# Two small reorderings in a two-block hybrid model: where 44 convolution taps stand, and how the first input arrives

## The chip, the cores and the metric

The kernel runs on one core of a Trainium2 chip. Five engines run side by side, each with its own list of instructions: TensorE (PE, with its weight loads shown as PEld), VectorE (DVE), ScalarE (ACT), GpSimd (POOL) and SyncE (SP), which here issues the transfers from the large memory. The metric is the time of one execution on the device in microseconds; lower is better. Three executions were timed, and the median counts.

## The reference, cut to what matters

Sequence length is 256, model width 1024, all in float32. Block 1 has two layers; each multiplies x by `w_in` (1024 x 4300 columns), runs three kinds of attention on the result, gates, and multiplies by `w_out`. Block 2 has two layers over 256 latent and 256 context tokens, and each layer adds three branches with their own gates: a convolution module, gated linear attention (GLA), and grouped attention.

```python
def hybrid_layer(x, w_in, ...):                      # block 1, two layers
    h = jnp.einsum('bsd,de->bse', x, w_in)           # the first product of the program
...
def conv_module(val, glu, gate, dw_w, dw_b, ln_g, ln_b, w_o):   # block 2
    u = val * jax.nn.sigmoid(glu)
    u = lax.conv_general_dilated(u, dw_w[:, None, :], ...,      # 31 taps, each channel for itself
                                 feature_group_count=D_CONV) + dw_b
    u = jax.nn.silu(layer_norm_2(u, ln_g, ln_b)) * jax.nn.silu(gate)
    return u @ w_o
```

The convolution has 512 channels and 31 taps. On the chip a tap is one elementwise instruction.

## The kernel before, in words

**Products.** Every float32 matrix is kept as a rounded high part and the rest (`h` and `l`), and a product is three TensorE instructions, h by h, h by l and l by h (`mm3`, lines 163 to 165). `WStream` brings the weights: `_dma` (L120, on SP) loads the next block in a fixed order, `_split` makes the high part on ACT (L133) and the rest on DVE (L134). The blocks are named after their columns: `0A` are the first 460 columns of block 1, layer 0, cut along the contraction at k-tiles `KA = (0, 1, 2, 4, 6, 8)` into five pieces of 1, 1, 2, 2, 2 k-tiles; `0B` is the next group.

**The start.** `load_x` (L1654) issues, for each of the five pieces, the part of x and then the part of `0A` that goes with it, ten transfers in all, of 128 to 512 KB. Behind each pair ACT casts x (`xTh`), then `0A` (`wh_0A`), and DVE makes `xTl` and `wl_0A`. The group A has 48 products of 460 columns: 8 k-tiles, two halves of the tokens, three products each. They start when the first piece has been cast. `setup1` then loads constants (`cst`), and the stream goes on with `0B`.

**The taps.** In block 2, `conv_taps` (L985) is a generator of 124 DVE instructions for a layer: 4 tiles of 128 channels, 31 taps each (L989 the first, L991 the rest), 128 x 512 in layer 0 and 128 x 256 in layer 1. `ucv` is their result. `some_taps(n, anchor)` takes the next n of them and lets them stand on DVE behind `anchor`. Who takes how many is set by two tables:

- `TAPS[l]`: behind each of the score steps of the attention in `scores` (L1033). Layer 0 has eight, so at 20 a step the 124 are used up there.
- `TAPG[l]`: four numbers, per gate of the attention branch (`ag`), per merge of that branch (`m3`/`oa`), per gate of the GLA branch (`gg`, in `gated`, L1256), and per merge of that branch (`m2`/`og`, behind L1291 or L1294).

What is left runs in `conv_finish`, whose transposes (`cvt`) need all of `ucv`.

**The order of layer 0 of block 2.** Attention (scores and weighing, one step per block of 128 tokens and key head), with gate products as filler on TensorE; the `ag` gates with outputs `yag`, and merges `m3`/`oa` (product `yoa`); GLA in two parts, for the context tokens (`gl00..`, `gn00..`) and the latent ones (`gl01..`, `gn01..`), moved up by a priority into the attention's tail; the `gg` gates with `ygg`; merges `m2`/`og` (product `yog`); convolution end; `cg` gates; merges `m1`/`oc`. A scheduler fixes each engine's list from the program's order and the priorities; the lists are then run in order.

Of the kernel before, what the change touches and what calls it, by code (L numbers as in the profile page):

```python
# [66 lines left out]
def units1o():  # L67
    return [(f'O{c}{j}', 2 * j, 2, [(512 * c, 512)]) for c in range(2) for j in range(4)]


def ncols(cols):
    return sum(n for _, n in cols)


def pack(w, units):
    parts = []
    for _, k0, kk, cols in units:
        blk = w.reshape(-1, 128, w.shape[1])[k0:k0 + kk]
# [22 lines left out]
class WStream:  # L101
# [12 lines left out]
    def _dma(self):  # L114
        i = self.nd
        self.nd += 1
        g = self.g
        key, src, off, kk, n = self.table[i]
        t = g.sp.tile([128, kk * n], F32, name=f'wr_{key}', tag='wraw', bufs=g.RAW)
        self.last = self.loads[key] = g.nc.sync.dma_start(t, src[off:off + 128 * kk * n].rearrange("(p n) -> p n", p=128))  # L120
        self.raw[i] = t
        if key in self.hooks:
            self.hooks.pop(key)()

    def _split(self):
        i = self.ns
# [607 lines left out]

TAPS = (20, 19)
TAPG = ((0, 15, 5, 4), (3, 3, 14, 10))


def mod_stream(g, l, W):
# [753 lines left out]
def xT_layout(x):  # L1495
    return np.ascontiguousarray(x.T.reshape(8, 128, 256).transpose(1, 0, 2)).reshape(128, 2048)


def host_arrays(inp):
    h = dict(xt=xT_layout(inp['x'][0]), xtok=inp['x'][0], ctxt=xT_layout(inp['ctx_2'][0]), cst=consts(CST),  # L1500
             par1=par1(inp), par2=par2(inp), rowp=rowpar(inp), wup=wup(inp))
    for i, lst in enumerate(CST1):
        h[f'cst1{i}'] = consts(lst)
    for l in range(2):
        h[f'w1_{l}'] = pack(inp['w_in'][l], units1())
# [18 lines left out]
def width(lst):  # L1524
    return sum(w for _, w in lst)


def setup(ctx, tc, ins):
    g = type('G', (), {})()
    nc = g.nc = tc.nc  # L1530
    g.tc = tc
    cp = g.cp = ctx.enter_context(tc.tile_pool(name="cst", bufs=1))
    g.pp = ctx.enter_context(tc.tile_pool(name="psum", bufs=4, space=PSUM))
    sp = g.sp = ctx.enter_context(tc.tile_pool(name="act", bufs=1))
    g.GM, g.AT, g.RAW, g.WB, g.ROW, g.K8, g.T2, g.UP, g.TE, g.TQ = KN
    g.k8 = lambda shape, name, dt=F32: sp.tile(shape, dt, name=name, tag='k8', bufs=g.K8)
    g.te = lambda shape, name, dt=F32: sp.tile(shape, dt, name=name, tag='te', bufs=g.TE)
    g.tq = lambda shape, name, dt=F32: sp.tile(shape, dt, name=name, tag='tq', bufs=g.TQ)
    g.t2 = lambda shape, name, dt=F32: sp.tile(shape, dt, name=name, tag='t2', bufs=g.T2)
    g.dram = ctx.enter_context(tc.tile_pool(name="dram", bufs=1, space=bass.MemoryType.DRAM))  # L1540
    nosync = mybir.DependencyInfo(mybir.DependencyClass.NoSync, mybir.DependencyReason.DATA)
    sync = mybir.DependencyInfo(mybir.DependencyClass.Sync, mybir.DependencyReason.DATA)
    g.wait = lambda a, b: tc.add_manual_dep(a.ins, b.ins.name, sync, reason="both in one go")
    g.after = lambda a, b: tc.add_manual_dep(a.ins, b.ins.name, nosync, reason="one engine, this order")
    c = cp.tile([128, width(CST)], F32, name="cst")
    g.load_cst = lambda: nc.sync.dma_start(c, ins['cst'])
    v = views(c, CST)
    g.idf, g.ones, g.sel8, g.hm, g.zc = v['ident'], v['ones'], v['sel8'], v['hm'], v['zc']
    g.gmask = v['gmask'].rearrange("p (a t) -> p a t", a=2)
    g.rope2c = v['rope2'].rearrange("p (a t d) -> p a t d", a=2, t=2)  # L1550
    g.idb = cp.tile([128, 128], BF, name="idb")
    return g


def setup1(g, ins, W):
# [3 lines left out]

    def load(nm, lst, more=0):  # L1560
        c = g.sp.tile([128, width(lst) + more], F32, name=nm, tag='up', bufs=g.UP)
        nc.sync.dma_start(c[:, 0:width(lst)], ins[nm])
        v.update(views(c, lst))
        return c

    c = load('cst10', CST1[0], 64)
    g.rope1 = v['rope1'].rearrange("p (t a d) -> p t a d", t=2, a=2)
    g.load_cst()
    nc.vector.tensor_copy(g.idb, g.idf)
    g.causal = c[:, width(CST1[0]):].bitcast(BF)  # L1570

# [80 lines left out]


def load_x(g, ins, W):  # L1654
    nc = g.nc
    x32 = g.k8([128, 8, 256], 'x0T')
    xTh = g.k8([128, 8, 256], 'xTh0', F32R)
    xTl = g.k8([128, 8, 256], 'xTl0', F32R)
    for a, b in zip(KA, KA[1:]):
        ks = slice(a, b)  # L1660
        nc.sync.dma_start(x32[:, ks], ins['xt'].rearrange("p (k t) -> p k t", k=8)[:, ks])
        W._dma()
        nc.scalar.copy(xTh[:, ks], x32[:, ks])
        W._split()
        nc.vector.tensor_sub(xTl[:, ks], x32[:, ks], xTh[:, ks].bitcast(F32))
    return xTh, xTl


# [21 lines left out]
def program(ctx, tc, ins, out, parts=(1, 2)):  # L1690
# [110 lines left out]
```

## Time and profile before

| what | value |
|---|---|
| median of 3 runs | 1201.55 us (1201.11, 1201.55 and 2284.37) |
| the profiled execution | 1202.12 us, its span 1200.3 us |
| PE busy | 1170.1 us, 97% of the span |
| PEld busy | 978.8 us, 82% |
| DVE busy | 919.0 us, 77% |
| ACT busy | 571.1 us, 48% |
| mean granted TensorE clock | 0.995 of full |
| chain that ended last | PE 75%, DVE 13%, DMA 5%, ACT 4%, issue 2% |

The span is cut into stretches, and in each the busy time of every engine is set against the stretch's length. Where TensorE is not busy, the timeline gives in square brackets how long it was idle ahead of an instruction and who ended the wait. The granted clock of a stretch stands as a share of full speed: 0.50 is 1.2 GHz and 1.00 is 2.4 GHz. Matmuls overlap, so the start of one to the start of the next tells their pace, not the duration shown.

### The profile page before, as it was taken

To read this page: it belongs to the slowest core of one execution; us is meant where nothing else is said; L and a number is where in the kernel's file an instruction comes from. 1 tells how busy PE (TensorE), PEld (TensorE's weight loads), DVE (VectorE), ACT (ScalarE), POOL (GpSimd) and SP (SyncE) were. 2 spreads that over 40 slices of the span, in tenths; PEclk is the share of its full clock that TensorE was granted. 3 is DMA by queue.
4 is the path that set the end of the run, shared out by engine and by line. 5 is a ranking of instruction groups with operands and counts; after the bars stand their busy time and mean duration, and the time that the engine had idled before them with its cause. 6 is when DMAs were issued, how large, how long until landed. Compare 5 with 4: busy or idle time off the path is not lost.

```text
span 1200.3 us, 20616 instructions
## 1 busy us (share of the span) xinstructions
PE 1170.1 (97%) x8012; PEld 978.8 (82%) x8012; DVE 919.0 (77%) x2050; ACT 571.1 (48%) x1024; POOL 11.2 (1%) x42
## 2 busy tenths in 40 slices
PE   8999999999999999999799999999999999999998
PEld 6888766677887777778578888888999778999998
DVE  6986766966799759999946544845799897896984
ACT  5556534456565433246254522433455533855552
POOL 0000000000000000000000000000000000000000
PEclk9999999999999999999899999999999999999999
DMA  7643566466555642131131332334655333544552
GB/s 258 230 126 121 191 202 227 166 211 201 188 189 205 197 140 71 44 115 37 57 119 54 93 101 88 88 105 158 177 159 170 110 106 112 187 160 124 176 176 71
DMA packets 48258, 171.33 MB, mean 143 GB/s; under 512 B 5340, under 2 KB 6492, under 8 KB 47392
## 3 DMA queue, kind: packets, MB, share of 16 engines
q1 hardware_dynamic: 48160, 170.01, 43.5%
q8 instruction: 63, 1.03, 0.3%
q14 instruction: 35, 0.29, 0.1%
HBM read 167.89 MB, written 2.10 MB: 142 GB/s over the span
## 4 chain that ended last, share of the span: by engine, by line
PE 75%; DVE 13%; DMA 5%; ACT 4%; issue 2%; SPq 0%; ACTq 0%; DVEq 0%
PE f0m L163 3%; PE f0m L165 3%; PE f0m L164 3%; PE f1m L165 2%; PE f1m L163 2%; PE f1m L164 2%; PE mod L749 1%; PE po L164 1%; PE po L165 1%; PE po L163 1%; PE go L165 1%; PE go L164 1%; PE go L163 1%; DVE ucv L991 1%; PE yog L165 1%
## 5 line engine op out<-in xcount | busy, mean ns | idle before, releaser
L991 DVE SCALAR_TENSOR_TENSOR ucv<-up,par,ucv 128x512 f32<-128x512 f32 (+1 forms) x240 | 146.9, 612 | 2.1
L165 PE MATMUL f0m<-hTh,wl_0m 128*128 128x512 f32 x192 | 75.4, 393 | 0.0
L163 PE MATMUL f0m<-hTh,wh_0m 128*128 128x512 f32 x192 | 75.3, 392 | 0.0
L164 PE MATMUL f0m<-hTl,wh_0m 128*128 128x512 f32 x192 | 75.2, 392 | 0.0
L163 PE MATMUL f1m<-hTh,wh_1m 128*128 128x256 f32 x192 | 54.9, 286 | 0.1
L165 PE MATMUL f1m<-hTh,wl_1m 128*128 128x256 f32 x192 | 54.8, 286 | 0.0
L164 PE MATMUL f1m<-hTl,wh_1m 128*128 128x256 f32 x192 | 54.5, 284 | 0.0
L133 ACT CAST wh_0m<-wr_0m 128x1024 fp32r<-128x1024 f32 x24 | 25.3, 1054 | 58.1 <-PE f0m L164 15.7
L134 DVE TENSOR_TENSOR wl_0m<-wr_0m,wh_0m 128x1024 fp32r<-128x1024 f32 x24 | 29.2, 1220 | 21.6 <-ACT wh_0m L133 21.5
L165 PEld LDWEIGHTS f0m<-hTh,wl_0m 128*128 128x128 f32 x192 | 36.2, 189 | 7.7 <-issue 0.2
L164 PEld LDWEIGHTS f0m<-hTl,wh_0m 128*128 128x128 f32 x192 | 36.2, 189 | 7.4
L163 PEld LDWEIGHTS f0m<-hTh,wh_0m 128*128 128x128 f32 x192 | 36.2, 189 | 7.4
L163 PEld LDWEIGHTS f1m<-hTh,wh_1m 128*128 128x128 f32 x192 | 36.8, 192 | 0.5 <-ACT wh_1m L133 0.3
L165 PEld LDWEIGHTS f1m<-hTh,wl_1m 128*128 128x128 f32 x192 | 36.7, 191 | 0.2 <-DVE wl_1m L134 0.2
L164 PEld LDWEIGHTS f1m<-hTl,wh_1m 128*128 128x128 f32 x192 | 36.8, 191 | 0.1
L133 ACT CAST wh_1m<-wr_1m 128x1024 fp32r<-128x1024 f32 x24 | 25.0, 1050 | 24.4 <-PE f1m L164 9.8
L134 DVE TENSOR_TENSOR wl_1m<-wr_1m,wh_1m 128x1024 fp32r<-128x1024 f32 x24 | 29.3, 1219 | 8.6 <-ACT wh_1m L133 8.4
L1278 ACT ACTIVATE mtm<-f0m,hbin 128x512 f32<-128x512 f32 x24 | 16.4, 682 | 9.3 <-DVE acc L1291 8.9
L134 DVE TENSOR_TENSOR wl_0o<-wr_0o,wh_0o 128x1024 fp32r<-128x1024 f32 x8 | 9.8, 1224 | 13.2 <-ACT wh_0o L133 13.2
L1392 DVE SCALAR_TENSOR_TENSOR xT<-po,mod,xT 128x256 f32<-128x256 f32 x16 | 7.7, 483 | 14.6 <-PE po L165 14.6
L164 PE MATMUL yoa<-yag,wh_0oa 128*128 128x512 f32 x32 | 13.2, 414 | 5.3 <-DVE yag L199 5.3
L164 PE MATMUL po<-mgl,wh_0o 128*128 128x256 f32 x64 | 18.2, 285 | 0.0
(1854 smaller groups left out, 3971.6 us busy)
## 6 DMA issues: line engine op xcount, KB each, us to landing
wr_0mod<-in_wm_dram SPq DMA_DIRECT2D x24, 512.0 KB, 4.4
wr_1mod<-in_wm_dram SPq DMA_DIRECT2D x24, 512.0 KB, 3.6
wr_0m<-in_w_dram SPq DMA_DIRECT2D x24, 512.0 KB, 3.5
wr_1m<-in_w_dram SPq DMA_DIRECT2D x24, 512.0 KB, 3.5
wr_0O<-in_w1o_dram SPq DMA_DIRECT2D x8, 512.0 KB, 3.6
wr_1O<-in_w1o_dram SPq DMA_DIRECT2D x8, 512.0 KB, 4.1
wr_0o<-in_wo_dram SPq DMA_DIRECT2D x8, 512.0 KB, 3.5
wr_0p<-in_wo_dram SPq DMA_DIRECT2D x8, 512.0 KB, 3.7
```

What stands on the lines that cost most here:

```text
L133: g.nc.scalar.copy(wh, r)
L134: g.nc.vector.tensor_sub(wl, r, wh.bitcast(F32))
L163: nc.tensor.matmul(out, lh, rh, start=start, stop=False)
L164: nc.tensor.matmul(out, lh, rl, start=False, stop=False)
L165: nc.tensor.matmul(out, ll, rh, start=False, stop=stop)
L749: nc.tensor.matmul(ps[32 * q:32 * q + 32], g.cz[:, k // 2, 2 * (k % 2):2 * (k % 2) + 32], w[:, 0, 256 * q:256 * q + 256], start=k == 0, st ...
L991: yield nc.vector.scalar_tensor_tensor(o, src, dw[:, i, j:j + 1], o, op0=OP.mult, op1=OP.add)
L1278: nc.scalar.activation(sg, pm, AF.Tanh, scale=0.5, bias=hb[:, blk(n, f)])
L1392: nc.vector.scalar_tensor_tensor(r[:, f, :], ps[:, :256], g.mod[l][:, 16 + f, w:w + 1], r[:, f, :], op0=OP.mult, op1=OP.add)
```

## The change: two tables of numbers, and another way in for the first input

First, `TAPS` for layer 0 of block 2 goes from 20 to 10 and its `TAPG` from (0, 15, 5, 4) to (0, 0, 6, 4). Layer 1 keeps its numbers. There are still 124 taps. Second, x and `0A` are packed on the host piece by piece into one array `xa`; `load_x` brings it in five transfers of 358, 358, 716, 716 and 716 KB, one behind the other in SP's list, into tiles of the pool `k8`, and `take()` hands the weights in them to the stream. The constants' loads are ordered behind them. Third, twelve bf16 products of 128 x 512 on a tile of zeros stand ahead of everything on TensorE; their result is read by nobody. A branch that the program never took is removed.

```diff
-TAPS = (20, 19)
-TAPG = ((0, 15, 5, 4), (3, 3, 14, 10))
+TAPS = (10, 19)
+TAPG = ((0, 0, 6, 4), (3, 3, 14, 10))
...
+def pack_xa(x, w):
+    parts = []
+    for _, k0, kk, cols in units1()[:len(KA) - 1]:
+        blk = pack(w, [('A', k0, kk, cols)]).reshape(128, -1)
+        parts.append(np.concatenate([blk, x[:, 256 * k0:256 * (k0 + kk)]], axis=1).reshape(-1))
+    return np.concatenate(parts)
...
+    def take(self, dma, r):
+        key = self.table[self.nd][0]
+        self.last = self.loads[key] = dma
+        self.raw[self.nd] = r
+        self.nd += 1
...
 def load_x(g, ins, W):
-    x32 = g.k8([128, 8, 256], 'x0T')
+    z = g.te([128, 512], 'z0', BF)
+    nc.vector.memset(z, 0.0)
+    pz = g.pp.tile([128, 512], F32, name='pz0', tag='at', bufs=g.AT)
+    for _ in range(12):
+        nc.tensor.matmul(pz, z[:, 0:128], z, start=True, stop=True)
...
-    for a, b in zip(KA, KA[1:]):
-        ks = slice(a, b)
-        nc.sync.dma_start(x32[:, ks], ins['xt'].rearrange("p (k t) -> p k t", k=8)[:, ks])
-        W._dma()
-        nc.scalar.copy(xTh[:, ks], x32[:, ks])
+    o = 0
+    for j, (a, b) in enumerate(zip(KA, KA[1:])):
+        ks, nw = slice(a, b), (b - a) * NA
+        n = nw + (b - a) * 256
+        r = g.k8([128, n], f'xa{j}')
+        d = nc.sync.dma_start(r, ins['xa'][o:o + 128 * n].rearrange("(p n) -> p n", p=128))
+        if j:
+            g.after(d, W.last)
+        W.take(d, r[:, 0:nw])
+        o += 128 * n
+        x32 = r[:, nw:n].rearrange("p (k t) -> p k t", t=256)
+        nc.scalar.copy(xTh[:, ks], x32)
         W._split()
-        nc.vector.tensor_sub(xTl[:, ks], x32[:, ks], xTh[:, ks].bitcast(F32))
+        nc.vector.tensor_sub(xTl[:, ks], x32, xTh[:, ks].bitcast(F32))
```

The lines move: L134 becomes L155, L199 L220, L991 L1012, L1142 L1163, L1180 L1201 and so on.

DVE, at the end of the attention of layer 0, before: the last `yag`, which `yoa` needs, stands between taps (L991) and the second half of the context GLA (`gl001..`).

```order
L1180 SCALAR_TENSOR_TENSOR sts_5657<-gw_0_5661,gl000dec,gl000c_6308 128x128
L991 SCALAR_TENSOR_TENSOR ucv_4999<-up_4597,par_1328,ucv_4999 128x512
L1137 COPY gl001last<-gl001cum 128x8
L991 SCALAR_TENSOR_TENSOR ucv_4999<-up_4597,par_1328,ucv_4999 128x512
L1142 TENSOR_TENSOR gl001ks_6341<-gl001last,gl001cum 128x512
L991 SCALAR_TENSOR_TENSOR ucv_4999<-up_4597,par_1328,ucv_4999 128x512
L199 SCALAR_TENSOR_TENSOR yag_0_5665<-qag_5663,yag_0_5664 128x512
L991 SCALAR_TENSOR_TENSOR ucv_4999<-up_4597,par_1328,ucv_4999 128x512
L1145 TENSOR_TENSOR gl001ks_6341<-gl001ks_6341,qkT_5380 128x512
```

After, on DVE around the last `yag` (now L220):

```order
L1172 TENSOR_TENSOR gl000ki_6259<-gl000ki_6259,qkT_5344 128x512
L220 SCALAR_TENSOR_TENSOR yag_0_5629<-qag_5627,yag_0_5628 128x512
L155 TENSOR_TENSOR wl_0oa_5897<-wr_0oa_5790,wh_0oa_5896 128x1024
L1198 COPY gw_0_5625<-gl000c_6271 128x256
L1201 SCALAR_TENSOR_TENSOR gw_0_5625<-gw_0_5625,gl000dec,gl000c_6272 128x128 x2
L1201 SCALAR_TENSOR_TENSOR gw_0_5625<-gw_0_5625,gl000dec,gl000c_6271 128x128 x2
L1201 SCALAR_TENSOR_TENSOR sts_5621<-gw_0_5625,gl000dec,gl000c_6272 128x128 x2
L1158 COPY gl001last<-gl001cum 128x8
L1163 TENSOR_TENSOR gl001ks_6305<-gl001last,gl001cum 128x512
L1166 TENSOR_TENSOR gl001ks_6305<-gl001ks_6305,qkT_5344 128x512
L1171 TENSOR_TENSOR gl001qi_6309<-gl001qi_6309,qkT_5344 128x512
```

The taps are gone from this place, and `yag` stands ahead of `gl001last`.

DVE in the `gg` gates, before: each gate is L1253, L1256 and L199, with a weight split (L134) between two gates and no tap.

```order
L1253 SCALAR_TENSOR_TENSOR qgg_6738<-gtgg_0_6772,qgg_6738 128x512
L1256 TENSOR_TENSOR qgg_6738<-qgg_6738,goT_6264 128x512
L199 SCALAR_TENSOR_TENSOR ygg_0_6740<-qgg_6738,ygg_0_6739 128x512
L134 TENSOR_TENSOR wl_0og_6858<-wr_0og_6741,wh_0og_6857 128x1024
L1253 SCALAR_TENSOR_TENSOR qgg_6738<-gtgg_0_6810,qgg_6738 128x512
L1256 TENSOR_TENSOR qgg_6738<-qgg_6738,goT_6264 128x512
L199 SCALAR_TENSOR_TENSOR ygg_0_6740<-qgg_6738,ygg_0_6739 128x512
L134 TENSOR_TENSOR wl_0m_2_6896<-wr_0m_2_6779,wh_0m_2_6895 128x1024
L1253 SCALAR_TENSOR_TENSOR qgg_6738<-gtgg_0_6848,qgg_6738 128x512
```

After, at the same gates:

```order
L1274 SCALAR_TENSOR_TENSOR qgg_6702<-gtgg_0_6736,qgg_6702 128x512
L1277 TENSOR_TENSOR qgg_6702<-qgg_6702,goT_6228 128x512
L220 SCALAR_TENSOR_TENSOR ygg_0_6704<-qgg_6702,ygg_0_6703 128x512
L1012 SCALAR_TENSOR_TENSOR ucv_5168<-up_4541,par_1337,ucv_5168 128x512 x3
L155 TENSOR_TENSOR wl_0og_6841<-wr_0og_6705,wh_0og_6840 128x1024
L1012 SCALAR_TENSOR_TENSOR ucv_5168<-up_4541,par_1337,ucv_5168 128x512
L1274 SCALAR_TENSOR_TENSOR qgg_6702<-gtgg_0_6780,qgg_6702 128x512
L1012 SCALAR_TENSOR_TENSOR ucv_5168<-up_4541,par_1337,ucv_5168 128x512
L1277 TENSOR_TENSOR qgg_6702<-qgg_6702,goT_6228 128x512
L1012 SCALAR_TENSOR_TENSOR ucv_5168<-up_4541,par_1337,ucv_5168 128x512
L220 SCALAR_TENSOR_TENSOR ygg_0_6704<-qgg_6702,ygg_0_6703 128x512
L1012 SCALAR_TENSOR_TENSOR ucv_5168<-up_4541,par_1337,ucv_5168 128x512
```

Six taps follow each gate's output, so they stand ahead of the next gate's.

SP at the start, before, from the ninth transfer on (`x0T` is the last part of x, `wr_0A_109` the last piece of `0A`; the eight ahead are the same pairs):

```order
L1661 DMA x0T<-in_xt_dram 128x512
L120 DMA wr_0A_109<-in_w_0_dram 128x920
L1562 DMA cst_117<-in_cst_dram 128x256
L1546 DMA cst<-in_cst_dram 128x782
L120 DMA wr_0B_145<-in_w_0_dram 128x1024
```

After, from the fourth on:

```order
L1691 DMA xa_110<-in_xa_dram 128x1432
L1691 DMA xa_118<-in_xa_dram 128x1432
L1583 DMA cst_126<-in_cst_dram 128x256
L1567 DMA cst<-in_cst_dram 128x782
L130 DMA wr_0B_154<-in_w_0_dram 128x1024
```

Five transfers (`xa`) stand where ten did, ahead of the same constants and the same `0B`.

## Rows read from the trace of the kernel before

**Rows 1.** the page, parts 1 and 4: busy time by engine; the chain of waits by engine

```profile
PE 1170.1 (97%) x8012; PEld 978.8 (82%) x8012; DVE 919.0 (77%) x2050; ACT 571.1 (48%) x1024; POOL 11.2 (1%) x42
...
PE 75%; DVE 13%; DMA 5%; ACT 4%; issue 2%; SPq 0%; ACTq 0%; DVEq 0%
```

**Rows 2.** stretches of the program: length, busy time (instructions) of each engine, PE clock, DMA share, GB/s

```profile
440.00:571.46 131.46, 131.45 (x985) 102.14 (x985) 125.30 (x212) 57.03 (x92) 3.25 (x7) 1.00 0.21 65
571.46:576.72 5.26, 0.00 (x1) 0.01 (x1) 5.26 (x12) 1.43 (x4) 0.00 (x0) 0.79 0.00 0
576.72:584.65 7.93, 7.68 (x74) 6.43 (x75) 7.93 (x13) 0.96 (x2) 0.00 (x0) 0.50 0.16 39
584.65:610.00 25.35, 21.61 (x166) 17.45 (x165) 20.66 (x40) 9.78 (x25) 0.17 (x2) 1.00 0.38 125
...
656.30:690.40 34.10, 33.77 (x153) 27.64 (x152) 18.89 (x32) 19.34 (x39) 0.00 (x0) 1.00 0.29 84
690.40:747.00 56.60, 56.60 (x258) 47.03 (x256) 22.65 (x26) 15.67 (x18) 0.00 (x0) 1.00 0.31 99
```

**Rows 3.** the timeline, TensorE's first products: start, us, engine line op out<-in [idle before <-releaser]

```profile
4.57 0.75 PE L163 MATMUL g0A<-wh_0A,xTh 128*128 128x460 f32 x1 [4.57 <-ACT wh_0A L133]
...
12.64 0.59 PE L165 MATMUL g0A<-wh_0A,xTl 128*128 128x460 f32 x1
...
13.79 0.59 PE L165 MATMUL g0A<-wh_0A,xTl 128*128 128x460 f32 x1
...
15.05 0.37 PE L165 MATMUL g0A<-wh_0A,xTl 128*128 128x460 f32 x1
...
20.43 0.37 PE L165 MATMUL g0A<-wh_0A,xTl 128*128 128x460 f32 x1
...
21.04 0.19 PEld L164 LDWEIGHTS g0B<-wl_0B,xTh 128*128 128x128 f32 x1 [0.21 <-DVE wl_0B L134]
```

**Rows 4.** the timeline, DVE and ACT at the start

```profile
0.84 0.17 DVE L1608 MEMSET cz<- 128x136 f32 x1 [0.84 <-PEq L1791]
...
13.72 0.96 ACT L133 CAST wh_0A<-wr_0A 128x920 fp32r<-128x920 f32 x1 [0.43 <-DMA wr_0A<-in_w_dram]
...
14.71 1.12 DVE L134 TENSOR_TENSOR wl_0A<-wr_0A,wh_0A 128x920 fp32r<-128x920 f32 x1 [0.19 <-ACT wh_0A L133]
```

**Rows 5.** stretches at the start, for the DMA columns at the right

```profile
4.00:7.00 3.00, 2.43 (x6) 1.78 (x6) 1.18 (x3) 0.90 (x3) 0.00 (x0) 1.00 0.83 180
...
2.00:13.70 11.70, 8.28 (x17) 5.31 (x18) 5.35 (x8) 5.45 (x10) 0.00 (x0) 1.00 0.94 310
```

**Rows 6.** the chain of waits at the attention's end: start, us, what

```profile
575.40 0.66 DVE ucv L991
576.06 0.60 DVE yag L199
```

**Rows 7.** the timeline, TensorE's stops at the attention's end

```profile
576.72 0.79 PE L164 MATMUL yoa<-yag,wh_0oa 128*128 128x512 f32 x1 [5.26 <-DVE yag L199]
...
584.65 0.44 PE L164 MATMUL f0m<-hTl,wh_0m 128*128 128x512 f32 x1
...
592.55 1.16 PE L1217 MATMUL gl00o<-gv,gl00am 128*128 128x128 f32 x8 [1.83 <-DVE gl00am L1209]
...
606.10 0.63 PE L1242 MATMUL gn00t<-cst,gw 128*128 128x128 f32 x4 [0.75 <-DVE gw L1239]
```

**Rows 8.** the timeline, the same step of the latent GLA, which has no taps

```profile
664.35 1.23 PE L1242 MATMUL gn01t<-cst,gw 128*128 128x128 f32 x8 [0.33 <-DVE gw L1239]
```

**Rows 9.** the timeline, DVE and PE in the gg gates and the first og merge

```profile
665.86 0.69 DVE L1253 SCALAR_TENSOR_TENSOR qgg<-gtgg,qgg 128x512 f32<-128x512 f32 x1
...
684.76 0.69 DVE L199 SCALAR_TENSOR_TENSOR ygg<-qgg,ygg 128x512 fp32r<-128x512 f32 x1 [0.70 <-ACT ygg L198]
...
691.31 0.39 PE L163 MATMUL yog<-ygg,wh_0og 128*128 128x512 f32 x1
...
694.23 0.69 DVE L1293 SCALAR_TENSOR_TENSOR mtm<-mtm,yog 128x512 f32<-128x512 f32 x1 [0.64 <-PE yog L165]
```

More of the change, by code (lines that the diff above doesn't have):

```diff
@@ L46 @@
 _A = 'dsa_q dsa_k idx_k dsa_v idx_w fox_f'.split()
+NA = 460
 SPL1 = dict(diff_q=(0, 512), diff_k=(512, 512), diff_v=(1024, 512), dsa_q=(1536, 256), dsa_k=(1792, 64),
@@ L119, in _dma @@
         t = g.sp.tile([128, kk * n], F32, name=f'wr_{key}', tag='wraw', bufs=g.RAW)
-        self.last = self.loads[key] = g.nc.sync.dma_start(t, src[off:off + 128 * kk * n].rearrange("(p n) -> p n", p=128))
+        d = g.nc.sync.dma_start(t, src[off:off + 128 * kk * n].rearrange("(p n) -> p n", p=128))
+        if i == len(KA) - 1:
+            g.after(d, self.last)
+        self.last = self.loads[key] = d
         self.raw[i] = t
@@ L123, in _dma @@
             self.hooks.pop(key)()
+    def take(self, dma, r):
[3 more added lines that the diff above has]
+        self.nd += 1
+        assert key not in self.hooks
     def _split(self):
@@ L1504, in host_arrays @@
     for l in range(2):
[L1505 removed]
+        h[f'w1_{l}'] = pack(inp['w_in'][l], units1()[0 if l else len(KA) - 1:])
         h[f'w1o_{l}'] = pack(inp['w_out'][l], units1o())
@@ L1545, in setup @@
     c = cp.tile([128, width(CST)], F32, name="cst")
-    g.load_cst = lambda: nc.sync.dma_start(c, ins['cst'])
+    g.load_cst = lambda after: g.after(nc.sync.dma_start(c, ins['cst']), after)
     v = views(c, CST)
@@ L1561, in load @@
         c = g.sp.tile([128, width(lst) + more], F32, name=nm, tag='up', bufs=g.UP)
-        nc.sync.dma_start(c[:, 0:width(lst)], ins[nm])
+        g.after(nc.sync.dma_start(c[:, 0:width(lst)], ins[nm]), W.last)
         v.update(views(c, lst))
@@ L1567, in setup1 @@
     g.rope1 = v['rope1'].rearrange("p (t a d) -> p t a d", t=2, a=2)
-    g.load_cst()
+    g.load_cst(W.last)
     nc.vector.tensor_copy(g.idb, g.idf)
@@ L1699, in program @@
         for l in range(2):
-            seq += table(ins[f'w1_{l}'], f'{l}', units1()) + table(ins[f'w1o_{l}'], f'{l}', units1o())
+            us = units1()
+            if l == 0:
+                seq += [(f'0{k}', None, 0, kk, ncols(c)) for k, _, kk, c in us[:len(KA) - 1]]
+                us = us[len(KA) - 1:]
+            seq += table(ins[f'w1_{l}'], f'{l}', us) + table(ins[f'w1o_{l}'], f'{l}', units1o())
     for l in range(2):
```

10 lines of the change are left out of this document (1 added, 9 removed).

## The prediction

> **What bounds the kernel now.** The page comes first: TensorE is busy for 1170.1 us of a span of 1200.3, and three quarters of the chain of waits are its own work, 13% DVE's [rows 1]. The change takes no product away (it adds twelve), so all it can win is time in which TensorE stands still or runs at the lower clock. The table of stretches says where that is. From 440 to 571.46 TensorE is dense, 131.45 of 131.46 us, while DVE works 125.30 of them, most of it taps. Then TensorE does nothing for 5.26 us, runs 7.93 us at a granted clock of 0.50, and is idle for 3.74 of the next 25.35 us [rows 2]. The timeline names who ends these stops: the first `yoa` product waits 5.26 us for the last `yag`, the next long ones are on `gl00am` (1.83 us) and, through ACT's statistics, on `gw` (0.75 us); all are DVE's [rows 7]. The chain shows what DVE did then: a tap (0.66 us), then `yag` (0.60), one tap between every two useful instructions [rows 6]. So at the attention's end DVE is behind, and taps are what it is behind with. The other place is the start, where TensorE's first product waits 4.57 us and then runs at the pace of the lower clock [rows 3].
>
> **Part 1, the taps.** None is removed: of layer 0's 124, 44 move. The order lists have 80 in the attention (before: all), 24 in the `gg` gates and 20 in the `og` merges. Between the last `rc` of the attention and the first `gl00am`, DVE's list has 36 taps before and 5 after. At 0.66 us each, as in the chain [rows 6], 31 taps are 20.5 us of DVE's time ahead of the work that TensorE waits for. The stops add up to 5.26 + 0.25 + 3.74 = 9.25 us [rows 2]; 20.5 us cover each of them.
>
> Behind the first stop the clock is down from 576.72 to 584.65, where it rises again [rows 2, 7]. At half speed 7.68 us of work cost about 3.8 us more than they need. Without the stop the clock has no cause to fall. The most that can come back is thus 9.25 + 3.8 = 13.1 us. What is late next is the group norm of the context GLA: its transposes wait for a chain ACT, DVE, TensorE that has no tap in it. The same step of the latent GLA, which runs without taps today, still shows 0.33 us of such a wait [rows 8] against 0.75 here [rows 7]. I leave 1.1 us standing for this and its like, and take **12.0 us**. The low end is 5.5: only the first stop and the 0.25 behind it go, the others stay, and one of them still brings the clock down.
>
> Where the 44 taps go, DVE works 18.89 of 34.10 us in the gates and 22.65 of 56.60 in the merges [rows 2]: 49.2 us free for 44 x 0.66 = 29.0 us. The cover is DVE's idle time, so the cost is **0**. Tightest are the gates. Four of them fill the 19.6 us from 665.86 to 685.45, where the last `ygg` ends, and the first `yog` product, which needs it, starts at 691.31 [rows 9], so there are 5.9 us of slack. In the new list 14 taps stand ahead of that last `ygg`, 9.2 us, of which most falls into the gaps between gates (a gate is three instructions of 0.69 and a weight split of about 1.2, scaled from 1.12 for 920 columns [rows 4]: 3.3 of some 5.5 us). By hand I place the last `ygg` some 2 us later than now, 4 us before it is needed. If the gaps gave nothing, TensorE would stand for 9.2 - 5.9 = 3.3 us there. In the merges the 20 taps and their drains fit well under the products. The convolution's own end needs its last tap only behind the merges, at 747.
>
> **Part 2, the start.** Twelve products of 512 columns on zeros run ahead of the first real one. DVE's own first instruction today is a memset at 0.84 that takes 0.17 us [rows 4]; the zeros' memset now precedes it, so I let the products begin at 1.2. In the trace 460 columns take (13.79 - 12.64)/3 = 0.383 us at the lower pace and (20.43 - 15.05)/26 = 0.207 at the full one, with 18 of the group's 48 products started by 13.79 [rows 3]. Scaled to 512 columns the zeros take 12 x 0.426 = 5.1 us and end at 6.3, against a first real product at 4.57 today: by themselves they cost 1.7 us. What they may buy is an earlier rise of the clock.
>
> The clock column reads 1.00 for the start's stretches [rows 5], though the pace there is half of what it is later, so I go by the pace. When it rises is bounded by two events. After the long stop it rose 7.9 us after TensorE had begun again (576.72 to 584.65) [rows 7]; at the start some 9.7 us after the first product (4.57 to about 14.3) [rows 3]. That gives 9.1 or 10.9 for a beginning at 1.2. The former stretch was dense, as the zeros are, while the start has waits of 0.4 to 0.7 us in it, so I take 9.1. Then 7 products run at 0.383 (6.3 to 9.1) and 41 at 0.207: the group ends at 17.6 instead of 20.64, 3.0 us earlier. With 10.9 it is 2.1.
>
> That holds if the data keep up. The same 2.93 MB of x and `0A` come in; from 2.0 to 13.7 the queues moved 310 GB/s with the constants among it [rows 5]. At that rate the last piece lands at 11.5 (today its cast starts at 13.72). The tail then takes ACT about 0.55 for x (scaled from 0.96 for 920 columns) and 0.96 for the weights, and DVE 1.12 [rows 4]: 14.1, and eleven more products make 16.4, ahead of 17.6. So TensorE sets the end. At the poorest rate, the 180 GB/s of 4 to 7 us [rows 5], the last piece lands at 18.3 and the group ends at 23.3, 2.7 us later than today; it is a remote end, since that stretch is three us of the twelve whose mean is 310. The best end has the clock up halfway through the zeros, which then stop near 5.4, and data faster than the mean: 48 x 0.207 = 9.9 behind it, 15.3, 5.3 us. I subtract 0.3 for `0B`, whose first low part TensorE already waits 0.21 us for [rows 3] and which the earlier end leaves less time. I take **2.7 us**, between -2.7 and 5.3.
>
> TensorE's rule in the Trainium skill (TensorE: Matmul & The Clock Gate, Part 1, What's actually happening) is that the lower clock is the default and activity releases it, at a point not tied to when the kernel starts, so that the number of slow products differs from run to run. The rows here have two different delays, 7.9 and 9.7 us, which agrees.
>
> **Sum.** The profiled execution took 1202.12 us (span 1200.3 and 1.8 around it), 0.6 above the median: 1202.1 - 12.0 - 2.7 - 0 = **1187.4**, so I say 1187.
>
> **Rivals.**
> - *The start gives nothing.* Zeros are no activity that raises the clock, or the merged pieces come late enough. For it: the zeros do delay the first product by 1.7 us. Against: they fill TensorE without a gap. Then 1190. Chance 0.13.
> - *The clock rises during the zeros.* If its moment is not tied to the start, it may come well before 9.1; with the best end above, 5.3 - 0.3 instead of 2.7: 1185. The page cited above bears on this. Chance 0.08.
> - *The attention keeps half of its stops.* The fillers that kept TensorE dense from 440 to 571.46 stand elsewhere relative to the shorter score steps, and TensorE waits there instead, for maxima and casts that no tap delays. For it: the eight steps of about 16 us each keep 10 taps, 6.6 us, and a scheduler moves TensorE's list along with DVE's. Against: 20.5 us is over twice the stops. Then 1193. Chance 0.12.
> - *The gates fall behind.* The last `ygg` comes 3.3 us late and the clock falls behind that stop, 4 us more: 1195. Against it are the 4 us of slack. Chance 0.08.
> - *Slower than before.* DVE cannot take taps in the gates and merges at all without holding up what follows, so that each moved tap is paid in full. From 14.7/0.66 = 22 taps on, half of the 44, the kernel is slower than before; with all, 1187 + 29 = 1216. Against: 49.2 us of idle time. Chance 0.03.
> - *The taps do not leave the attention*, because the scheduler places them there anyway: the new list has 5 where 36 were, so 0.01.
>
> The forecast has 0.55. From 1185 to 1195 lie nearly all of these; with the bounds of the two unknown sizes the range is **1182 to 1197**. A change of under 2%, 24 us, cannot be told from none by a measurement of this kernel: faster than 1177.5 needs more than all that the rows offer (1202.1 - 13.1 - 5.3 = 1183.7), 0.02; slower than 1225.6 more than every tap exposed, 0.01; the rest, 0.97, is within.
>
> **What would show it.** In the new profile: no stop of several us ahead of the first `yoa` product and no stretch at 0.50 behind it; idle time between 570 and 610 of about 1 us; the tap rows of the `gg` gates between `ygg` rows, with the first `yog` product bound by TensorE. At the start twelve products from about 1.2, the pace doubling near 9, the first `0B` product near 17.6. Wrong would be a stop ahead of `yog`, DVE waits inside the score steps, or a group A that waits for its transfers.

## The result, and the profile after

The changed kernel takes **1190.83 us** (median of 4 runs, 1189.63 to 1192.62). Set against the kernel before, the ratio is **0.988, interval 0.984 to 0.992**: 1.2% faster, clear of noise but inside the 2% that count as the same. The ratio is of undisturbed runs, so one run of the kernel before, of 2284.37 us, is not in it. The forecast was 1187, the range 1182 to 1197. The profiled execution is the slowest of the four, 1192.62 us with a span of 1190.8, against 1202.12 and 1200.3.

The page after, parts 1 and 4, answers to [rows 1]: TensorE's busy time is 1.6 us less, although it has twelve products more.

```profile
PE 1168.5 (98%) x8024; PEld 975.7 (82%) x8024; DVE 921.1 (77%) x2051; ACT 569.5 (48%) x1024; POOL 11.2 (1%) x42
...
PE 76%; DVE 11%; DMA 6%; ACT 5%; issue 2%; SPq 0%; ACTq 0%; DVEq 0%
```

**Where the 9.5 us went.** The span is cut at three marks found in both traces: the first product of `g0B`, of `f0GQ` and of `gl010cum`.

| stretch | before | after | gained |
|---|---|---|---|
| start to `g0B` | 20.64 | 19.90 | 0.74 |
| `g0B` to `f0GQ`, not touched by the change | 429.75 | 432.13 | -2.38 |
| `f0GQ` to `gl010cum`, the attention and the context GLA | 179.54 | 168.80 | 10.74 |
| `gl010cum` to the end, with the `gg` gates and `og` merges | 570.37 | 569.97 | 0.40 |

**The attention.** The stretches of the changed kernel (length, busy time and instructions of PE, PEld, DVE, ACT, POOL, clock, DMA share, GB/s) answer to [rows 2].

```profile
440.00:565.00 125.00, 124.19 (x950) 94.58 (x949) 113.71 (x189) 55.60 (x90) 3.23 (x7) 1.00 0.25 79
565.00:610.00 45.00, 44.22 (x327) 36.65 (x326) 22.38 (x46) 16.36 (x35) 0.00 (x0) 1.00 0.23 70
650.00:690.40 40.40, 40.08 (x181) 32.89 (x180) 37.33 (x61) 19.09 (x35) 0.00 (x0) 1.00 0.30 92
690.40:747.00 56.60, 56.60 (x260) 46.80 (x259) 40.92 (x81) 14.60 (x17) 0.17 (x2) 1.00 0.30 93
```

TensorE's idle time from 440 to 610 is 1.6 us where it was 9.3, and no stretch is at 0.50. DVE, which was idle for half of the gates and merges, now works 37.33 of 40.40 and 40.92 of 56.60 us there, while TensorE stays at 40.08 and 56.60. The timeline has two stops left before 610, answering to [rows 7]: one in the score steps, new, and the group norm's, as it was.

```profile
542.26 0.50 PE L1066 MATMUL at031e<-at031q,k 128*128 128x512 f32 x1 [0.78 <-ACT at031x L1069]
...
590.46 0.63 PE L1263 MATMUL gn00t<-cst,gw 128*128 128x128 f32 x4 [0.68 <-DVE gw L1260]
```

In the gates the last `ygg` ends at 678.0, 4.2 us ahead of the first `yog` product [rows 9]. That first product reads the first gate's output, though. A `yog` group has twelve products, three for each of the four gates' outputs; the eleventh, at 684.45, is the first that reads DVE's part of the last `ygg`, so 6.4 us are left:

```profile
677.34 0.69 DVE L220 SCALAR_TENSOR_TENSOR ygg<-qgg,ygg 128x512 fp32r<-128x512 f32 x1
...
682.18 0.39 PE L184 MATMUL yog<-ygg,wh_0og 128*128 128x512 f32 x1
...
684.45 0.39 PE L185 MATMUL yog<-ygg,wh_0og 128*128 128x512 f32 x1
```

**The start.** TensorE's timeline answers to [rows 3], ACT's row to [rows 4].

```profile
1.19 4.33 PE L1683 MATMUL pz<-z 128*128 128x512 bf16 x12 [1.19 <-DVE z L1680]
5.17 0.76 PE L184 MATMUL g0A<-wh_0A,xTh 128*128 128x460 f32 x2
...
7.65 0.37 PE L186 MATMUL g0A<-wh_0A,xTl 128*128 128x460 f32 x1
10.02 0.69 PE L184 MATMUL g0A<-wh_0A,xTh 128*128 128x460 f32 x2 [2.00 <-ACT wh_0A L154]
11.17 0.72 PE L185 MATMUL g0A<-wl_0A,xTh 128*128 128x460 f32 x1 [0.46 <-DVE wl_0A L155]
...
14.38 0.50 PE L184 MATMUL g0A<-wh_0A,xTh 128*128 128x460 f32 x1
```

```profile
8.49 0.62 ACT L1697 CAST xTh<-xa 128x512 fp32r<-128x512 f32 x1 [2.58 <-DMA xa<-in_xa_dram]
```

Twelve zeros take 3.98 us (1.19 to 5.17), so the last of them run at the full pace already, and the first real products come 0.207 us apart. At 8.02 TensorE is through the first two pieces; the third is cast only from 8.49. It waits 2.00 us and, behind two products, 0.46. Then the clock is down, and the table of stretches shows it:

```profile
8.02:10.02 2.00, 0.00 (x0) 0.00 (x0) 0.71 (x2) 1.48 (x2) 0.00 (x0) 1.00 1.01 413
11.17:14.38 3.21, 3.21 (x9) 2.80 (x10) 3.00 (x4) 2.10 (x3) 0.00 (x0) 0.51 1.03 412
```

What the zeros won is spent again at 0.51, some 1.6 us in 3.2.

### The profile page after: what moved, and what is told of

It reads as the page before. It is cut to its first block, busy times and chain, and to the rows that moved or that the text cites. A ratio compares the mean times of both kernels' runs of the same rounds, so it can differ in the third digit from the quotient of the medians.

```text
span 1190.8 us, 20632 instructions
## 1 busy us (share of the span) xinstructions
PE 1168.5 (98%) x8024; PEld 975.7 (82%) x8024; DVE 921.1 (77%) x2051; ACT 569.5 (48%) x1024; POOL 11.2 (1%) x42
## 4 chain that ended last, share of the span: by engine, by line
PE 76%; DVE 11%; DMA 6%; ACT 5%; issue 2%; SPq 0%; ACTq 0%; DVEq 0%
PE f0m L186 3%; PE f0m L185 3%; PE f0m L184 3%; PE f1m L186 2%; PE f1m L184 2%; PE f1m L185 2%; PE po L185 1%; PE po L186 1%; PE po L184 1%; PE mod L770 1%; PE go L186 1%; PE go L185 1%; PE go L184 1%; PE yog L186 1%; PE yoc L186 1%
## 5 line engine op out<-in xcount | busy, mean ns | idle before, releaser
L1012 DVE SCALAR_TENSOR_TENSOR ucv<-up,par,ucv 128x512 f32<-128x512 f32 (+1 forms) x240 | 147.3, 614 | 2.8
L155 DVE TENSOR_TENSOR wl_0m<-wr_0m,wh_0m 128x1024 fp32r<-128x1024 f32 x24 | 29.3, 1222 | 18.2 <-ACT wh_0m L154 18.1
L155 DVE TENSOR_TENSOR wl_1m<-wr_1m,wh_1m 128x1024 fp32r<-128x1024 f32 x24 | 29.3, 1221 | 8.6 <-ACT wh_1m L154 8.4
L155 DVE TENSOR_TENSOR wl_0o<-wr_0o,wh_0o 128x1024 fp32r<-128x1024 f32 x8 | 9.8, 1224 | 13.2 <-ACT wh_0o L154 13.2
L186 PE MATMUL pp<-mgh,wl_0p 128*128 128x256 f32 x64 | 18.2, 284 | 0.0
L185 PE MATMUL pp<-mgl,wh_0p 128*128 128x256 f32 x64 | 18.2, 284 | 0.0
```

The lines of the kernel that those rows point to most:

```text
L155: g.nc.vector.tensor_sub(wl, r, wh.bitcast(F32))
L185: nc.tensor.matmul(out, lh, rl, start=False, stop=False)
L186: nc.tensor.matmul(out, ll, rh, start=False, stop=stop)
L1012: yield nc.vector.scalar_tensor_tensor(o, src, dw[:, i, j:j + 1], o, op0=OP.mult, op1=OP.add)
```

## The experiments

Every ratio is to the kernel before on the same chip. "Taps" counts those on DVE between the last `rc` (the reciprocal of the last score step) and the last `yag`; the wait is the longest of TensorE inside group A behind its first product; the last column is `f0GQ` to `gl010cum`. All but the medians and ratios come from one profiled execution each. A dash is no wait of 0.2 us or more.

| kernel | median, ratio [interval] | wait | `g0B` | taps | stretch |
|---|---|---|---|---|---|
| before | 1202.7 to 1205.4 (five medians) | 0.4 | 20.64 | 24 | 179.5 |
| changed | 1190.83, 0.988 [0.984, 0.992] | 2.0 | 19.90 | 5 | 168.8 |
| e1 tables only | 1193.59, 0.992 [0.989, 0.994] | 0.7 | 19.26 | 5 | 170.0 |
| e2 start only | 1204.32, 1.001 [0.999, 1.003] | 1.1 | 17.97 | 24 | 179.6 |
| e3 no zeros | 1190.25, 0.990 [0.988, 0.991] | - | 16.98 | 5 | 169.1 |
| e4 24 zeros | 1192.14, 0.991 [0.989, 0.992] | - | 18.25 | 5 | 169.2 |
| e5 zeros, ten transfers | 1195.53, 0.992 [0.990, 0.995] | 1.3 | 20.56 | 5 | 170.6 |
| e6 14 taps a step | 1199.46, 0.995 [0.993, 0.997] | 1.1 | 18.10 | 24 | 176.8 |
| e7 44 taps in the gates | 1193.15, 0.991 [0.988, 0.994] | 1.3 | 18.44 | 5 | 169.3 |
| e8 5 taps a step | 1201.38, 0.998 [0.997, 1.000] | 2.4 | 20.27 | 0 | see e8 |
| e9 13 taps a step, no zeros | 1188.43, 0.987 [0.985, 0.990] | - | 17.52 | 17 | 168.1 |
| e10 8 zeros | 1191.26, 0.989 [0.988, 0.991] | 1.7 | 17.97 | 5 | 169.0 |
| e11 no zeros, old tables | 1202.91, 0.998 [0.997, 0.999] | 0.6 | 18.48 | 24 | 182.4 |
| e12 third piece halved | 1189.60, 0.988 [0.985, 0.990] | - | 17.62 | 17 | 168.1 |

### e1: the tables alone

The changed tables in the kernel before.

```diff
-TAPS = (20, 19)
-TAPG = ((0, 15, 5, 4), (3, 3, 14, 10))
+TAPS = (10, 19)
+TAPG = ((0, 0, 6, 4), (3, 3, 14, 10))
```

> The two tables as changed, the start as before (ten transfers, no products on zeros). My theory, read from the two traces: nearly all of the gain is the taps'. From TensorE's 450 to 630 us the changed kernel wins 10.7 us, so about 11 us of the whole here, 1190 to 1192 where before is 1202, with the first 0B product at 20.6 as before. The changed kernel's trace also shows 2.4 us lost between 20 and 450 us, in code that the change did not touch; if that is the start's doing, it is gone here, and the time is nearer 1189. Rival: the start gives more of the whole than its 0.7 us at the first 0B product, and this run gains clearly under 9 us.

The stretch of the attention is won (170.0); the whole, 1193.59, is 1.6 us above the expected range. The loss between `g0B` and `f0GQ` is there too, 433.4 us, with the start of before: the changed start is not needed for it. Over the traces this untouched stretch takes 428.6 to 435.0 us (e8, whose `f0GQ` moved, left out). Two parts can be read. TensorE's waits in it add up to 8.4 us before, 9.8 in the changed kernel, 10.1 here, and 6.9 (e11) to 11.4 (e12) over all traces, most of them for ACT and DVE. And from 200 to 300 us, in block 1, this execution and e12 have a mean clock of 0.98.

`g0B` starts at 19.26 here and at 20.64 in the trace of before, with the same start. In before products become 0.207 us apart only from 14.85 on, here they are 0.21 apart by 11.84, so the 20.64 that the start is compared with came from a late rise of the clock.

### e2: the start alone

The changed `load_x`, the old tables.

> The start as changed (five merged transfers, twelve products on zeros), the tables as before. My theory: the first 0B product starts at 19.9 instead of 20.64, because group A runs out of data at about 8 us, waits some 2 us for the third piece, and the clock falls behind that wait; the rest is as before, so 0 to 1.5 us gained, 1201 where before is 1202, and the stop of 5.3 us ahead of yoa with the clock at 0.50 behind it is still there. Rival: the merged start delays later loads of block 1, and the run is 1 to 2 us slower than before.

The whole does not move, as expected, and the stop is there to the digit:

```profile
574.92 0.79 PE L185 MATMUL yoa<-yag,wh_0oa 128*128 128x512 f32 x1 [5.26 <-DVE yag L220]
```

`g0B` came at 17.97, not at 19.9. Here the third piece was cast 0.35 us earlier and the first real product started 0.55 us later, so the wait was 1.10 instead of 2.00, and no clock fell behind it:

```profile
9.67 0.69 PE L184 MATMUL g0A<-wh_0A,xTh 128*128 128x460 f32 x2 [1.10 <-ACT wh_0A L154]
```

So the changed start has two outcomes 2 us apart, and the whole shows neither.

### e3: no products on zeros

```diff
-    for _ in range(12):
-        nc.tensor.matmul(pz, z[:, 0:128], z, start=True, stop=True)
```

> The changed kernel without the twelve products on zeros; merged transfers and both tables stay. My theory: the clock is released by TensorE's activity whatever it multiplies, so without the zeros the twelve first products of group A run at half pace from about 4.5, TensorE reaches the third piece at about the time it lands (9 to 10 us), waits little, and the rise comes at 13 to 14.5 us as before: first 0B product at 19.5 to 20.5, within 0.7 us of the changed kernel's 19.9. The zeros would then buy almost nothing here. Rival: the zeros are what gains at the start, and 0B comes 1.5 us or more later than 19.9.

The expectation missed on the better side: `g0B` starts at 16.98, earlier than in any run with zeros.

```profile
4.70 0.75 PE L184 MATMUL g0A<-wh_0A,xTh 128*128 128x460 f32 x1 [4.70 <-ACT wh_0A L154]
...
16.98 0.63 PE L184 MATMUL g0B<-wh_0B,xTh 128*128 128x512 f32 x2
```

The products are 0.38 us apart up to about 9.0 and 0.21 from 9.24 on, so the clock rose some 4 us sooner than was expected from the trace of before, and at half pace the first pieces last just until the third is there. The time of the whole is that of the changed kernel. The zeros buy nothing here.

### e4: 24 products on zeros

> The changed kernel with 24 products on zeros instead of 12. My theory: twelve end at 5.17, the second twelve run at the full pace and end at about 7.9, the first two pieces' twelve products (2.5 us) then last until 10.4, past the cast of the third piece at 9.97, so the stop of 2.0 us goes, the clock does not fall again, and group A ends at about 18.2: first 0B product at 18.2 instead of 19.9, about 1.5 us faster than the changed kernel as a whole. Rival: the clock falls for another reason than that stop (at the third piece's two halves, or by itself), and 0B comes at 20 or later because the first real product is 2.7 us later.

```profile
1.19 7.01 PE L1683 MATMUL pz<-z 128*128 128x512 bf16 x24 [1.19 <-DVE z L1680]
7.85 0.56 PE L184 MATMUL g0A<-wh_0A,xTh 128*128 128x460 f32 x1
...
18.25 0.63 PE L184 MATMUL g0B<-wh_0B,xTh 128*128 128x512 f32 x2
```

The wait and the fall of the clock are gone and `g0B` is at 18.25, as worked out; but the whole is no faster. 1.7 us at the start are below what these runs can tell apart.

### e5: zeros ahead of the ten transfers

The tables of the change, `load_x` of before with the lines of the zeros ahead of its loop.

> The tables as changed, the start of before (ten transfers) with the twelve products on zeros ahead of it. Theory after the first four runs: the zeros raise the clock early, but TensorE then eats the pieces faster than they come and waits; the group's end is set by the last piece, so 0B starts at 18 to 20 us, with one or more waits of 1 us and longer inside group A, no better than without the zeros (19.3 and 20.6 in the two runs with this start), and the whole is 1190 to 1195. Rival: the zeros alone are worth their purpose, the pace is full from about 5 us on, and 0B starts before 18.

Much as the theory had it, just beyond its far end: `g0B` at 20.56, a wait of 1.3 us, 1195.53 for the whole. From 11.89 to 15.00 the clock is at 0.50.

```profile
10.74 0.68 PE L163 MATMUL g0A<-wh_0A,xTh 128*128 128x460 f32 x2 [1.32 <-ACT wh_0A L133]
```

### e6: 14 taps behind a score step

```diff
+TAPS = (14, 19)
+TAPG = ((0, 0, 3, 1), (3, 3, 14, 10))
```

> The changed kernel with 14 taps behind each score step instead of 10 (20 before) and 3 instead of 6 in each gg gate: 25 taps stand on DVE between the last rc and the first gl00am, where before has 36 and the changed kernel 5. Theory: what cost time was DVE's backlog in front of yag. 11 taps fewer are 7.3 us less, more than the stop of 5.3 us, so the stop goes and the clock does not fall; of the later stops up to 2 us may stay. From f0GQ to gl010cum (179.5 us before, 168.8 after) 169 to 171.5 us; the whole within 2 us of the changed kernel. Rival: the gain goes with the number of taps taken away, 11 of 31: 175.7 us in that stretch, and the whole 6 to 7 us slower than the changed kernel.

The theory missed; the stop is there unchanged, and the rival's number (175.7) is nearer to the 176.8 measured.

```profile
577.01 0.79 PE L185 MATMUL yoa<-yag,wh_0oa 128*128 128x512 f32 x1 [5.26 <-DVE yag L220]
```

DVE's timeline shows why. The taps still stand one to one with the useful work up to `yag`; behind it there is a single one left.

```profile
575.61 0.74 DVE L1012 SCALAR_TENSOR_TENSOR ucv<-up,par,ucv 128x512 f32<-128x512 f32 x1
576.27 0.68 DVE L220 SCALAR_TENSOR_TENSOR yag<-qag,yag 128x512 fp32r<-128x512 f32 x1
576.87 0.74 DVE L1012 SCALAR_TENSOR_TENSOR ucv<-up,par,ucv 128x512 f32<-128x512 f32 x1
577.53 0.69 DVE L1166 TENSOR_TENSOR gl001ks<-gl001ks,qkT 128x512 f32<-128x512 f32 x1
```

Of the 36 taps that the prediction counted, 24 stand ahead of the last `yag` and 12 behind it, and the 11 taken away here were all from the 12. They are worth the 2.7 us that the stretch is shorter, the later stops. The first stop and the clock behind it belong to the 24.

### e7: all 44 taps in the gates, ahead of the next output

```diff
-TAPG = ((0, 0, 6, 4), (3, 3, 14, 10))
+TAPG = ((0, 0, 11, 0), (3, 3, 14, 10))
...
+                newest[0] = t
...
+        so = split_out(g, y[0][:, f, :], y[1][:, f, :], q[:, f, :], scale)
+        if l == 0 and ntaps > 10 and f:
+            g.after(so, newest[0])
```

> The changed kernel with all 44 moved taps in the gg gates, eleven behind each gate's output, and an order that keeps them ahead of the next gate's output: 33 taps stand ahead of the last ygg (14 in the changed kernel), none is left for the merges. This is the rival of the prediction in which moved taps are paid in full. Theory: a gate's DVE work becomes 3.3 + 11 x 0.66 = 10.6 us against TensorE's 5.5, so the last ygg comes about 14 us later than in the kernel before's pattern; 4 to 6 us of it are slack and the scheduler puts 18 products of the next m2 block ahead of the rest of yog, so TensorE stops for 5 to 9 us ahead of yog and the clock falls behind the stop: 1198 to 1206. Rival: DVE's idle time and TensorE's other work still cover it, and the time is within 2 us of the changed kernel's.

`newest[0]` is the tap issued last, so eleven taps stand ahead of each next output. The delay came as worked out, and the cost did not: the last `ygg` is 16.3 us later than in the changed kernel, and TensorE does not stop.

```profile
693.67 0.68 DVE L220 SCALAR_TENSOR_TENSOR ygg<-qgg,ygg 128x512 fp32r<-128x512 f32 x1
```

```profile
686.43 0.39 PE L184 MATMUL yog<-ygg,wh_0og 128*128 128x512 f32 x1
694.41 0.50 PE L185 MATMUL yog<-ygg,wh_0og 128*128 128x512 f32 x1
```

The scheduler's order allows for the late `ygg`. It has 33 products of the next `m2` gates between the parts of `yog`, and the first that needs the last `ygg` starts 0.06 us behind its end. The median is 2.3 us above the changed kernel's, the intervals overlap, and the stretch from `gl010cum` to the end takes 571.0 us against 570.0. The rival that each moved tap is paid in full is refuted for 44 taps.

### e8: 5 taps behind a score step

```diff
+TAPS = (5, 19)
+TAPG = ((0, 0, 11, 5), (3, 3, 14, 10))
```

> The changed kernel with 5 taps behind each score step, 11 in each gg gate where the scheduler finds room (14 stand ahead of the last ygg, as in the changed kernel) and 5 per og merge: 40 in the attention, 84 behind it. Theory: the attention has no stop left to win, 84 taps are 55 us and DVE's idle time in gates and merges was 49 us before any tap, so the convolution's transposes wait for the last taps: TensorE stops there for 4 to 12 us, and the kernel is 5 to 12 us slower than the changed one, 1195 to 1203. Rival: the attention still gains from fewer taps (f0GQ to gl010cum under 168), and the time is equal or better.

With 84 taps behind the attention the cover is gone. The last tap runs until 754.7 (723 in the changed kernel), the transposes wait 0.55 us for it, and what follows on DVE holds TensorE up once more and lets the clock fall:

```profile
754.72 0.55 PE L1337 MATMUL cvt<-cst,ucv 128*128 128x128 f32 x3 [0.55 <-DVE ucv L1012]
...
775.26 0.76 PE L184 MATMUL f0m<-hTh,wh_0m 128*128 128x512 f32 x1 [5.86 <-DVE gtcg L1285]
```

```profile
760.00:780.00 20.00, 13.44 (x59) 10.53 (x58) 18.28 (x39) 7.33 (x10) 0.45 (x6) 0.83 0.25 78
```

The whole is 1201.38, 10.6 us above the changed kernel. Somewhere between 44 and 84 taps the move thus begins to be paid. The attention gains nothing more: `f0GQ` moved in this program's order, and from `at000s` to `gl010cum` it takes 184.1 us against 184.6 with 10 taps a step.

### e9: 13 taps behind a score step

```diff
+TAPS = (13, 19)
+TAPG = ((0, 0, 5, 1), (3, 3, 14, 10))
```

> 13 taps behind each score step, 5 in each gg gate, the merged start without the products on zeros. In the trace of the run with 14 taps, 24 taps still ran between the last rc and the last yag, as many as before; the 11 taken away had all stood behind that yag. Here 17 stand ahead of it and none behind. Theory: what counts is the taps ahead of the last yag: 7 fewer are 4.6 us, the stop ahead of yoa shrinks from 5.3 to under 1 us, the clock does not fall, and from f0GQ to gl010cum it takes 168.5 to 170.5 us (before 179.5, with 14 taps 176.8, with 10 168.8). Rival: the gain comes from TensorE's own new order at 10 taps a step, or goes with the number of taps taken out, and it stays at 174 or more. At the start: 0B at 17 to 18 us, as in the first run without zeros (17.0).

168.1 us: with 17 taps ahead of the last `yag` instead of 24 the stop, the fallen clock and the later stops are gone (a wait of 0.54 us for a weight split is left at 570.66), and all that the change won in the attention is won. From the last score step to that `yoa` product TensorE's list has the same blocks of products, in the same order and with the same counts, as before and in e6, so a new order on TensorE is not what removes the stop here.

```profile
560.00:575.00 15.00, 14.46 (x149) 11.37 (x147) 14.31 (x26) 6.00 (x11) 0.00 (x0) 1.00 0.15 41
575.00:590.00 15.00, 14.95 (x136) 12.44 (x133) 9.76 (x18) 4.69 (x15) 0.00 (x0) 1.00 0.53 171
```

DVE is still busy there (14.31 of 15 us), but no longer late. The median, 1188.43, is the lowest of all; its interval overlaps that of the changed kernel.

### e10: 8 products on zeros

> The changed kernel with 8 products on zeros instead of 12. They end at about 4.6 us, when the first real product could start anyway (4.7 without zeros), so they cost nothing. Theory: the clock rises at 4 to 6 us, TensorE is through the first two pieces by about 7.5 us and waits for the third, 1.5 to 2.5 us; 0B starts between 17.5 and 20, later than without zeros (17.0), since what the zeros win early is given back as the wait, and twice so if the clock falls behind it. Rival: zeros that cost no delay gain what the clock gives, and 0B starts at 16.5 or earlier.

As expected: zeros that cost no delay are followed by a wait of 1.70 us, and `g0B` is at 17.97.

```profile
4.74 1.14 PE L184 MATMUL g0A<-wh_0A,xTh 128*128 128x460 f32 x2
...
9.68 0.69 PE L184 MATMUL g0A<-wh_0A,xTh 128*128 128x460 f32 x2 [1.70 <-ACT wh_0A L154]
```

### e11: the merged transfers alone

> Both tables as before, the merged start without products on zeros. Theory: the merged transfers are the part of the new start that helps, since the pieces land about a microsecond and a half earlier each: 0B at 17 to 18.5 us against 19.3 and 20.6 with ten transfers; the attention's stop of 5.3 us is there as before. 1199 to 1203 where before is 1203 to 1205. Rival: the 17.0 of the first run without zeros was a lucky moment of the clock, and 0B starts at 19 or later here.

18.48, at the late end, because the third piece came late (cast at 8.65, against 7.14 in e3 and 7.67 in e9). The attention has its stop of 5.26 us. Its stretch is 2.9 us longer than before because the clock fell twice: to 0.50 for 9.1 us behind that stop, and again to 0.50 from 590.0 to 599.5, behind a wait of 1.29 us for `gl00am`. In before a wait of 1.83 us at the same place was followed by a clock of 1.00 [rows 2, 7].

### e12: the third piece halved

```diff
-KA = (0, 1, 2, 4, 6, 8)
+KA = (0, 1, 2, 3, 4, 6, 8)
```

> The kernel with 13 taps and no products on zeros, with the group A cut at k-tiles 1, 2, 3, 4, 6, so that the third piece of 716 KB becomes two of 358 KB (layer 1's group A is cut the same way). In ten runs with merged transfers the first 0B product started 9.83 to 9.86 us after ACT's first cast of the third piece (eight runs), or 11.3 to 11.4 after it (the two in which the clock fell behind the wait), with and without products on zeros. Theory: the third piece is thus the bound of the start; halved, it is cast at 6.5 to 7.5, the next bound is the last piece (cast at 11 to 12, then 2.6 us of casts and eleven products, 2.3), and 0B starts at 16 to 17 us: a gain of 0.5 to 1.5 us over the run with 13 taps (17.5), too little for the whole time to show. Rival: the fixed distance is TensorE's own pace, and 0B stays at 17.5 or later.

The data came as early as the theory said, and `g0B` did not; the rival holds, at 17.62. With nothing to wait for, TensorE went at half pace until about 10.5.

```profile
5.92 0.41 ACT L1692 CAST xTh<-xa 128x256 fp32r<-128x256 f32 x1 [0.34 <-DMA xa<-in_xa_dram]
```

```profile
9.79 0.91 PE L184 MATMUL g0A<-wh_0A,xTh 128*128 128x460 f32 x2
10.54 0.37 PE L185 MATMUL g0A<-wl_0A,xTh 128*128 128x460 f32 x1
```

Behind the third piece as a bound stands the moment of the clock. Products on zeros in front of this version were not tried.

## Why the prediction was right, and where it was not

**The whole.** 1190.8 lies in the range and the sign is right, 4 us short of the forecast. The taps did what the forecast says; the start did what the rival "the start gives nothing" says (1190), by its second condition, pieces that come late enough. The profiled execution is 5.2 us above the sum, and the pair of traces puts 1.3 of them on the attention, 2.0 on the start and 2.4 on a stretch that the change does not touch, less 0.4 won behind it. How near the number came is in part luck: that stretch moves by more than the start's whole term from one trace to another, and the sum starts from an execution of 1202.1, where the kernel before has medians of 1202.7 to 1205.4.

**The attention, 12.0 forecast, 10.7 measured.** The place, the waits and the clock were read rightly, and so was the rest that would stay (0.68 at `gn00t`). The 0.78 at `at031e` in the score steps was not in the sum; it is the rival on the score steps in small. The size holds too: the first stop, the 0.25 behind it and the clock are 9.3 us in the sum, and e9 takes 8.7 less than e6, which has them. The count was too coarse. "20.5 us cover each of them" took the taps up to the first `gl00am` as one backlog; e6 and e9 show that the 5.3 us stop and the clock hang on the taps ahead of the last `yag`. Taking 7 of those 24 away (e9) does what taking 19 does, and taking 11 behind them (e6) leaves the stop standing.

**The gates and merges, 0 forecast, 0 measured** (0.4 gained in the last stretch). The last `ygg` ended 4.2 us ahead of the first `yog` product where the hand-sum had 4. But "the first `yog` product, which needs it" was misread: the first to read the last `ygg` is the eleventh, so before had 8.1 us of slack and not 5.9 (685.45 to 693.57), the changed kernel 6.4. e7 shows it: twenty `yog` products run ahead of the last `ygg`. The bound of 3.3 us and the rival "the gates fall behind" also overlooked that TensorE's list is made by the same scheduler: e7 delayed `ygg` by 16.3 us and TensorE did not stop. Idle DVE time agrees with the runs as a limit for the whole: 44 taps (29 us) fit the 49 us, and 84 (55 us) cost 10 us (e8).

```profile
693.57 0.39 PE L164 MATMUL yog<-ygg,wh_0og 128*128 128x512 f32 x1
```

**The start, 2.7 forecast, 0.7 in the trace.** This is the term that failed, at the step "TensorE sets the end": only the last piece was held against TensorE's pace, at a rate averaged over all. The third piece is what comes late, and "a group A that waits for its transfers", which the prediction named as a sign of being wrong, is what the trace shows. In eight of the ten runs with five merged transfers `g0B` starts 9.83 to 9.86 us behind its first cast, with 0, 8, 12 or 24 zeros; in the other two, the changed kernel and e8, 11.3 to 11.4 us behind it. Those are the two with waits of 2.0 and 2.4 us, and in both the clock is at half pace behind the wait. The 9.84 is the casts of that piece (with two products among them) and 34 products at 0.207 (7.04). The clock did rise earlier than I took it to, at about 4 instead of 9.1 (twelve zeros in 3.98 us, some six of them at 0.43 and the rest at 0.23), but products that run sooner only wait sooner. Neither of its two delays was typical of a start: in the other five traces without zeros (e1, e3, e9, e11, e12) the pace was full 4.5 to 7.2 us after the first product at the latest, where the trace of before shows 9.7, and the 7.9 is that of a long stop. (With 9.7 the prediction's sum gives 2.3 us, not the 2.1 written.) Over the five traces with the changed start `g0B` is at 18.9 on average, against 20.0 over the two of before: about 1 us. e2 against before (1.001 [0.999, 1.003]) shows that it is not seen in the whole. Without the zeros the merged transfers alone are just seen: e11 is at 0.998 [0.997, 0.999], 2.3 us in the medians.

**What stays open.** The untouched stretch takes 428.6 to 435.0 us from one trace to another, more than the start is worth. It goes with TensorE's waits for ACT and DVE in it and, in e1 and e12, with a fallen clock; why these differ between executions is not shown. Nor is it shown why the clock fell behind some waits of 1.3 us and not behind others of 1.7 and 1.8.

## What to carry to other kernels

When work is moved off a late engine, count what stands ahead of each instruction that is waited for, instruction by instruction; a total over the stretch hides that one stop, with the clock behind it, owns most of the loss (8.7 of 11 us here). Warming the clock ahead of the first product pays only if the operands then keep up: compare every piece's landing with the faster pace, not the last one's. And a filler's new place can be free while the engine's idle time there exceeds it (29 us into 49 here, not 55), all the more where a scheduler moves the consumer too.

## What was not expected of the hardware

- A stop of 5.3 us ahead of `yoa` was each time followed by a stretch at half the clock (0.50 for 7.9 us before, 9.0 in e6, 9.1 in e11 and 10.8 in e2), and the waits of 2.0 and 2.4 us at the start by one at 0.50 or 0.51; waits of 1.1 to 1.7 us there (e2, e6, e7, e10) were not. In e5 a wait of 1.3 us was, and in e11 one of 1.29 us ahead of `gl00o`.
- Products on zeros raised the pace like any other: in the five runs with the changed start the first real product came 3.98 to 4.74 us behind the first of twelve zeros, where twelve at half pace would take 5.1, so the rise came at a different product each time. That agrees with the Trainium skill's page TensorE: Matmul & The Clock Gate (Part 1, What's actually happening): activity releases the clock, at a moment not tied to the kernel's start.
- The piece that is third in the queue was first cast anywhere from 7.14 to 8.98 us in ten runs of the same five transfers.
